# Row-wise cosine similarity: loading the last tiles in chunks and storing the result as transposed rows

## The chip, the cores and the metric

The kernel runs on one core of a Trainium2 chip. The metric is the device time of one execution in microseconds, given as the median over the executions of a kernel. It is about 1.8 us longer than the span of the same execution in the profile (before: profiled run 1284.43 us, span 1282.6 us); the span is what the profile's views divide up.

## The reference

```python
def setup_inputs():
    return {"x": np.random.randn(8192, 8192).astype(np.float32),
            "y": np.random.randn(8192, 8192).astype(np.float32)}

def reference(x, y):
    x_norm = np.linalg.norm(x, axis=1, keepdims=True)
    y_norm = np.linalg.norm(y, axis=1, keepdims=True)
    return np.sum(x * y, axis=1) / (x_norm.squeeze() * y_norm.squeeze() + 1e-8)
```

Each of 8192 rows gives one number. 537 MB are read and 32 KB are written.

## The kernel before

The rows are cut into 64 tiles of 128 rows, one row per partition. Each tile of x and of y is one 4 MB load. ScalarE squares and sums x and y, and VectorE multiplies and sums x·y. Each tile leaves one column of `sxx`, `syy` and `sxy`. At the end a short chain turns the three [128x64] arrays into results, and one DMA stores them. In that store, neighbouring elements of a partition lie 128 elements apart in memory, so it consists of 8192 pieces of four bytes.

```python
    data = ctx.enter_context(tc.tile_pool(name="data", bufs=2))
    ...  # cut: other pools, sxx, syy, sxy [128, 64], bf16 scratch
    for i in range(ntiles):
        xt = data.tile([P, D], fp32)
        yt = data.tile([P, D], fp32)
        nc.sync.dma_start(out=xt, in_=x[i * P : (i + 1) * P, :])
        nc.sync.dma_start(out=yt, in_=y[i * P : (i + 1) * P, :])
        nc.scalar.activation(out=act_scr, in_=xt, func=Square, accum_out=sxx[:, i : i + 1])
        nc.scalar.activation(out=act_scr, in_=yt, func=Square, accum_out=syy[:, i : i + 1])
        nc.vector.tensor_tensor_reduce(out=dve_scr, in0=xt, in1=yt, ..., accum_out=sxy[:, i : i + 1])
    ...  # cut: den = sxx*syy; sqrt; +1e-8; reciprocal; res = sxy*rec, all [128, 64]
    out_v = out.rearrange("(i p) -> p i", p=P)
    nc.sync.dma_start(out=out_v, in_=res)
```

Of the kernel before, what the change touches and what calls it, by code (L numbers as in the profile page):

```python
# [1 line left out]

# [4 lines left out]


@with_exitstack
def kernel(  # L10
    ctx: ExitStack,
    tc: tile.TileContext,
    x: bass.AP,
    y: bass.AP,
    out: bass.AP,
):
    nc = tc.nc
    P = nc.NUM_PARTITIONS
    N, D = x.shape
    ntiles = (N + P - 1) // P  # L20
    assert N % P == 0

    fp32 = mybir.dt.float32
    bf16 = mybir.dt.bfloat16

    data = ctx.enter_context(tc.tile_pool(name="data", bufs=2))
    scratch = ctx.enter_context(tc.tile_pool(name="scratch", bufs=1))
    stats = ctx.enter_context(tc.tile_pool(name="stats", bufs=1))

    sxx = stats.tile([P, ntiles], fp32)  # L30
    syy = stats.tile([P, ntiles], fp32)
    sxy = stats.tile([P, ntiles], fp32)

    act_scr = scratch.tile([P, D], bf16)
    dve_scr = scratch.tile([P, D], bf16)

    for i in range(ntiles):
        xt = data.tile([P, D], fp32)
        yt = data.tile([P, D], fp32)
        nc.sync.dma_start(out=xt, in_=x[i * P : (i + 1) * P, :])  # L40
        nc.sync.dma_start(out=yt, in_=y[i * P : (i + 1) * P, :])  # L41

        nc.scalar.activation(  # L43
            out=act_scr,
            in_=xt,
            func=mybir.ActivationFunctionType.Square,
            accum_out=sxx[:, i : i + 1],
        )
        nc.scalar.activation(  # L49
            out=act_scr,  # L50
            in_=yt,
            func=mybir.ActivationFunctionType.Square,
            accum_out=syy[:, i : i + 1],
        )
        nc.vector.tensor_tensor_reduce(  # L55
            out=dve_scr,
            in0=xt,
            in1=yt,
            scale=1.0,
            scalar=0.0,  # L60
            op0=mybir.AluOpType.mult,
            op1=mybir.AluOpType.add,
            accum_out=sxy[:, i : i + 1],
        )

    den = stats.tile([P, ntiles], fp32)
    nc.vector.tensor_tensor(out=den, in0=sxx, in1=syy, op=mybir.AluOpType.mult)  # L67
    sden = stats.tile([P, ntiles], fp32)
    nc.scalar.activation(  # L69
        out=sden, in_=den, func=mybir.ActivationFunctionType.Sqrt  # L70
    )
    sdene = stats.tile([P, ntiles], fp32)
    nc.vector.tensor_single_scalar(  # L73
        out=sdene, in_=sden, scalar=1e-8, op=mybir.AluOpType.add
    )
    rec = stats.tile([P, ntiles], fp32)
    nc.vector.reciprocal(out=rec, in_=sdene)  # L77
    res = stats.tile([P, ntiles], fp32)
    nc.vector.tensor_tensor(out=res, in0=sxy, in1=rec, op=mybir.AluOpType.mult)  # L79

    out_v = out.rearrange("(i p) -> p i", p=P)
    nc.sync.dma_start(out=out_v, in_=res)


# [1 line left out]
_INS = ['x', 'y']  # L86
_OUTS = [((8192,), 'float32')]


# [23 lines left out]
```

## Time and profile before

| | before |
|---|---|
| median (first 4 runs) | 1284.81 us |
| span of the profiled run | 1282.6 us |
| last y tile lands | 1248.4 us |
| from there to the end (the tail) | 34.2 us |

These are lines of the profile's page of the kernel before: busy time of the engines, packets, the load queue, the chain that ended last, the largest group of VectorE, and the output store with its median time from issue to landing. (Issue is the moment at which an engine hands a DMA over, landing the moment at which its last completion signal arrives; a packet is one piece of it, here one row of a load or one element of the old store.)

```profile
DVE 557.9 (43%) x132; ACT 914.5 (71%) x259; POOL 0.2 (0%) x4
...
DMA packets 26648, 536.97 MB, mean 419 GB/s; under 512 B 10257, under 2 KB 10257, under 8 KB 10257
...
q1 hardware_dynamic: 26640, 536.91, 99.0%
...
DMA 75%; DVE 22%; SPq 1%; issue 1%; DVEq 0%; ACT 0%
...
L55 DVE CUSTOM_DVE_ANT_0 dve_scr<-xt,yt 128x8192 bf16<-128x8192 f32 x64 | 556.3, 8692 | 700.5 <-DMA yt<-in_y_dram 700.5
...
out_dram<-res SPq DMA_DIRECT2D x1, 32.0 KB, 23.0
```

Neither compute engine is near its limit; the DMA engines are. The table by stretches of the span (columns: stretch, length, busy time of DVE, ACT and POOL, clock, DMA share, GB/s) shows where the load stream runs and where it doesn't:

```profile
20.00:600.00 580.00, 261.00 (x60) 423.55 (x120) 0.00 (x0) 1.00 1.00 432
600.00:1200.00 600.00, 269.70 (x62) 438.56 (x125) 0.00 (x0) 1.00 1.00 432
...
1248.50:1282.60 34.10, 9.81 (x6) 8.66 (x4) 0.00 (x0) 1.00 0.65 1
```

For 1180 us the stream is saturated at 432 GB/s. In the last 34 us the DMA engines are busy 65% of the time and move 1 GB/s: that is the output store. The timeline (start, duration, engine, line, operation, and in brackets the idle time before it with its releaser) shows what the tail is made of:

```profile
1248.60 8.69 DVE L55 CUSTOM_DVE_ANT_0 dve_scr<-xt,yt 128x8192 bf16<-128x8192 f32 x1 [10.93 <-DMA yt<-in_y_dram]
1255.66 1.28 ACT L69 ACT_TABLE_LOAD   x1
1257.21 0.22 DVE L67 TENSOR_TENSOR den<-sxx,syy 128x64 f32<-128x64 f32 x1
...
1258.57 0.23 DVE L79 TENSOR_TENSOR res<-sxy,rec 128x64 f32<-128x64 f32 x1
1258.82 0.41 SPq L82 DMA_DIRECT2D out_dram<-res  x1
```

### The profile page before, as it was taken

What the parts mean: (1) busy time and instruction counts of PE and PEld (TensorE: products, weight loads), DVE (VectorE), ACT (ScalarE), POOL (GpSimd) and SP (SyncE); (2) the same over time, 40 slices, a digit from 0 to 9 for tenths busy, and PEclk for the clock granted to TensorE, in tenths of its full rate; (3) what the DMA queues carried; (4) which work ended last, traced back from release to release, by engine and by line L of the source; (5) the groups of instructions that cost most, each with busy time, mean ns of one, the idle gap of its engine ahead of it and who ended that gap; (6) DMA issues with size and microseconds to landing.
All of it is one profiled execution on the core that took longest, in us unless ns stands there. A gap on an engine that the chain in (4) does not pass through costs nothing.

```text
span 1282.6 us, 881 instructions
## 1 busy us (share of the span) xinstructions
DVE 557.9 (43%) x132; ACT 914.5 (71%) x259; POOL 0.2 (0%) x4
## 2 busy tenths in 40 slices
DVE  2345344354354353453453453543543534534532
ACT  4777777677677767767777776776777777677672
POOL 0000000000000000000000000000000000000000
DMA  9999999999999999999999999999999999999986
GB/s 409 425 441 425 434 432 427 438 426 435 431 430 434 427 437 429 430 434 427 440 426 432 433 427 439 426 436 430 426 439 426 438 427 430 436 427 436 428 364 1
DMA packets 26648, 536.97 MB, mean 419 GB/s; under 512 B 10257, under 2 KB 10257, under 8 KB 10257
## 3 DMA queue, kind: packets, MB, share of 16 engines
q1 hardware_dynamic: 26640, 536.91, 99.0%
q14 instruction: 8, 0.06, 0.0%
HBM read 536.87 MB, written 0.03 MB: 419 GB/s over the span
## 4 chain that ended last, share of the span: by engine, by line
DMA 75%; DVE 22%; SPq 1%; issue 1%; DVEq 0%; ACT 0%
DMA yt<-in_y_dram 75%; DVE dve_scr L55 22%; SPq L40 1%; DVEq L55 0%; SPq L41 0%; DVE sxy L55 0%; DVE rec L77 0%; ACT sden L69 0%; DVE res L79 0%; DVE sdene L73 0%; DVE den L67 0%
## 5 line engine op out<-in xcount | busy, mean ns | idle before, releaser
L55 DVE CUSTOM_DVE_ANT_0 dve_scr<-xt,yt 128x8192 bf16<-128x8192 f32 x64 | 556.3, 8692 | 700.5 <-DMA yt<-in_y_dram 700.5
L43 ACT ACTIVATE act_scr<-xt 128x8192 bf16<-128x8192 f32 x64 | 449.9, 7029 | 175.9 <-DMA xt<-in_x_dram 175.9
L49 ACT ACTIVATE act_scr<-yt 128x8192 bf16<-128x8192 f32 x64 | 449.9, 7030 | 166.1 <-DMA yt<-in_y_dram 166.1
L49 ACT ACTIVATION_READ_ACCUMULATOR act_scr<-yt 128x1 f32 x64 | 11.9, 186 | 0.0
L43 ACT ACTIVATION_READ_ACCUMULATOR act_scr<-xt 128x1 f32 x64 | 11.9, 186 | 0.0
L55 DVE DVE_READ_ACCUMULATOR2_ANT sxy<- 128x1 f32 x64 | 5.3, 83 | 0.0
L43 ACT ACT_TABLE_LOAD x1 | 1.3, 1283 | 0.7 <-PEq L97 0.7
L69 ACT ACT_TABLE_LOAD x1 | 1.3, 1283 | 0.0
L69 ACT ACTIVATE sden<-den 128x64 f32<-128x64 f32 x1 | 0.3, 256 | 0.5 <-DVE den L67 0.5
L77 DVE RECIPROCAL rec<-sdene 128x64 f32<-128x64 f32 x1 | 0.6, 554 | 0.0
L73 DVE TENSOR_SCALAR sdene<-sden 128x64 f32<-128x64 f32 x1 | 0.2, 194 | 0.3 <-ACT sden L69 0.3
L79 DVE TENSOR_TENSOR res<-sxy,rec 128x64 f32<-128x64 f32 x1 | 0.2, 225 | 0.0
L67 DVE TENSOR_TENSOR den<-sxx,syy 128x64 f32<-128x64 f32 x1 | 0.2, 219 | 0.0
L97 POOL MEMSET const-bfloat16-1.0<- 128x1 bf16 x1 | 0.1, 101 | 0.0
L97 POOL MEMSET const-uint8-127<- 128x1 uint8 x1 | 0.1, 101 | 0.0
L97 POOL MEMSET const-float32-0.0<- 128x1 f32 x1 | 0.1, 98 | 0.2 <-issue 0.2
L97 POOL MEMSET const-float32-1.0<- 128x1 f32 x1 | 0.1, 98 | 0.0
## 6 DMA issues: line engine op xcount, KB each, us to landing
xt<-in_x_dram SPq DMA_DIRECT2D x64, 4096.0 KB, 20.2
yt<-in_y_dram SPq DMA_DIRECT2D x64, 4096.0 KB, 29.5
out_dram<-res SPq DMA_DIRECT2D x1, 32.0 KB, 23.0
```

What stands on the lines that cost most here:

```text
L40: nc.sync.dma_start(out=xt, in_=x[i * P : (i + 1) * P, :])
L43: nc.scalar.activation(out=act_scr, in_=xt, func=mybir.ActivationFunctionType.Square, accum_out=sxx[:, i : i + 1],)
L49: nc.scalar.activation(out=act_scr, in_=yt, func=mybir.ActivationFunctionType.Square, accum_out=syy[:, i : i + 1],)
L55: nc.vector.tensor_tensor_reduce(out=dve_scr, in0=xt, in1=yt, scale=1.0, scalar=0.0, op0=mybir.AluOpType.mult, op1=mybir.AluOpType.add, ac ...
L67: nc.vector.tensor_tensor(out=den, in0=sxx, in1=syy, op=mybir.AluOpType.mult)
L69: nc.scalar.activation(out=sden, in_=den, func=mybir.ActivationFunctionType.Sqrt)
L73: nc.vector.tensor_single_scalar(out=sdene, in_=sden, scalar=1e-8, op=mybir.AluOpType.add)
L77: nc.vector.reciprocal(out=rec, in_=sdene)
L79: nc.vector.tensor_tensor(out=res, in0=sxy, in1=rec, op=mybir.AluOpType.mult)
L97: nc = _bacc.Bacc("TRN2", target_bir_lowering=False, num_devices=1)
```

## The change

Its intent is to shorten what follows the last load. The last tile is loaded and reduced in chunks of 2048, 2048, 2048, 1024 and 1024 columns (the one before it in two halves), so that little work is left when the last bytes land. The first 63 result columns are finished, transposed on TensorE and stored while the last tile loads. At the end only one column remains; it is transposed into one 512-byte row. A first square root on ScalarE makes it load the activation table once, at the start.

```diff
+    def chunks_of(t):
+        plan = {ntiles - 2: [4096, 4096],
+                ntiles - 1: [2048, 2048, 2048, 1024, 1024]}
+        ...
+    def emit_early():                      # columns 0..62
+            ...                            # the same chain as before, 63 wide
+            nc.tensor.transpose(res_t_ps, res[:, 0:M], ident)
+            nc.vector.tensor_copy(out=res_t, in_=res_t_ps)
+            nc.sync.dma_start(out=out_v[0:M, :], in_=res_t)
 ...
+        for (s, e) in bnds:
+            nc.sync.dma_start(out=xt[:, s:e], in_=x[t * P : (t + 1) * P, s:e])
+            yq.dma_start(out=yt[:, s:e], in_=y[t * P : (t + 1) * P, s:e])
+        if t == ntiles - 1:
+            emit_early()
+        if first:
+            make_identity(nc, ident)
+            nc.vector.memset(warm, 1.0)
+            nc.scalar.sqrt(out=warm, in_=warm)
+        for k, (s, e) in enumerate(bnds):
+            ...                            # squares and product per chunk, partial sums in csxx, csyy, csxy
 ...
+    nc.vector.reduce_sum(out=a, in_=csxx[:, c0:c1], axis=mybir.AxisListType.X)
+    ...                                    # csyy, csxy; the chain on [128, 1] -> res1
+    nc.tensor.transpose(row_ps, res1, ident)
+    nc.vector.tensor_copy(out=row, in_=row_ps)
+    nc.scalar.dma_start(out=out_v[t : t + 1, :], in_=row)
-    out_v = out.rearrange("(i p) -> p i", p=P)
-    nc.sync.dma_start(out=out_v, in_=res)
```

More of the change, by code (lines that the diff above doesn't have):

```diff
@@ L5 @@
 from concourse import bass_utils, mybir
+from concourse.masks import make_identity
 from concourse._compat import with_exitstack
@@ L24 @@
     bf16 = mybir.dt.bfloat16
+    AX = mybir.AluOpType
+    def chunks_of(t):
+        plan = {
+            ntiles - 2: [4096, 4096],
+            ntiles - 1: [2048, 2048, 2048, 1024, 1024],
+        }
+        ws = plan.get(t, [D])
+        assert sum(ws) == D
+        bounds = []
+        s = 0
+        for w in ws:
+            bounds.append((s, s + w))
+            s += w
+        return bounds
+    consts = ctx.enter_context(tc.tile_pool(name="consts", bufs=1))
     data = ctx.enter_context(tc.tile_pool(name="data", bufs=2))
@@ L28 @@
     stats = ctx.enter_context(tc.tile_pool(name="stats", bufs=1))
+    psum = ctx.enter_context(tc.tile_pool(name="psum", bufs=1, space=bass.MemoryType.PSUM))
     sxx = stats.tile([P, ntiles], fp32)
@@ L32 @@
     sxy = stats.tile([P, ntiles], fp32)
+    NCH = 24
+    csxx = stats.tile([P, NCH], fp32)
+    csyy = stats.tile([P, NCH], fp32)
+    csxy = stats.tile([P, NCH], fp32)
     act_scr = scratch.tile([P, D], bf16)
     dve_scr = scratch.tile([P, D], bf16)
-    for i in range(ntiles):
+    ident = consts.tile([P, P], fp32)
+    warm = consts.tile([1, 1], fp32)
+    out_v = out.rearrange("(i p) -> i p", p=P)
+    coff = {}
+    off = 0
+    for t in range(ntiles):
+        b = chunks_of(t)
+        if len(b) > 1:
+            coff[t] = off
+            off += len(b)
@@ new lines @@
+    assert off <= NCH
+    def emit_early():
+            M = ntiles - 1
+            den = stats.tile([P, ntiles], fp32)
+            nc.vector.tensor_tensor(out=den[:, 0:M], in0=sxx[:, 0:M], in1=syy[:, 0:M], op=AX.mult)
+            sden = stats.tile([P, ntiles], fp32)
+            nc.scalar.activation(out=sden[:, 0:M], in_=den[:, 0:M], func=mybir.ActivationFunctionType.Sqrt)
+            rec = stats.tile([P, ntiles], fp32)
+            nc.vector.tensor_single_scalar(out=rec[:, 0:M], in_=sden[:, 0:M], scalar=1e-8, op=AX.add)
+            nc.vector.reciprocal(out=rec[:, 0:M], in_=rec[:, 0:M])
+            res = stats.tile([P, ntiles], fp32)
+            nc.vector.tensor_tensor(out=res[:, 0:M], in0=sxy[:, 0:M], in1=rec[:, 0:M], op=AX.mult)
+            res_t_ps = psum.tile([M, P], fp32)
+            nc.tensor.transpose(res_t_ps, res[:, 0:M], ident)
+            res_t = stats.tile([M, P], fp32)
+            nc.vector.tensor_copy(out=res_t, in_=res_t_ps)
+            nc.sync.dma_start(out=out_v[0:M, :], in_=res_t)
@@ L38 @@
+    first = True
+    for t in range(ntiles):
         xt = data.tile([P, D], fp32)
         yt = data.tile([P, D], fp32)
-        nc.sync.dma_start(out=xt, in_=x[i * P : (i + 1) * P, :])
-        nc.sync.dma_start(out=yt, in_=y[i * P : (i + 1) * P, :])
-        nc.scalar.activation(
-            out=act_scr,
-            in_=xt,
-            func=mybir.ActivationFunctionType.Square,
-            accum_out=sxx[:, i : i + 1],
-        )
-        nc.scalar.activation(
-            out=act_scr,
-            in_=yt,
-            func=mybir.ActivationFunctionType.Square,
-            accum_out=syy[:, i : i + 1],
-        )
@@ L55 @@
-        nc.vector.tensor_tensor_reduce(
-            out=dve_scr,
-            in0=xt,
-            in1=yt,
-            scale=1.0,
-            scalar=0.0,
-            op0=mybir.AluOpType.mult,
-            op1=mybir.AluOpType.add,
-            accum_out=sxy[:, i : i + 1],
-        )
-    den = stats.tile([P, ntiles], fp32)
-    nc.vector.tensor_tensor(out=den, in0=sxx, in1=syy, op=mybir.AluOpType.mult)
-    sden = stats.tile([P, ntiles], fp32)
-    nc.scalar.activation(
-        out=sden, in_=den, func=mybir.ActivationFunctionType.Sqrt
-    )
@@ L72 @@
-    sdene = stats.tile([P, ntiles], fp32)
-    nc.vector.tensor_single_scalar(
-        out=sdene, in_=sden, scalar=1e-8, op=mybir.AluOpType.add
-    )
-    rec = stats.tile([P, ntiles], fp32)
-    nc.vector.reciprocal(out=rec, in_=sdene)
-    res = stats.tile([P, ntiles], fp32)
-    nc.vector.tensor_tensor(out=res, in0=sxy, in1=rec, op=mybir.AluOpType.mult)
-    out_v = out.rearrange("(i p) -> p i", p=P)
-    nc.sync.dma_start(out=out_v, in_=res)
+        bnds = chunks_of(t)
+        yq = nc.sync
@@ new lines @@
+        for (s, e) in bnds:
[4 more added lines that the diff above has]
+        if first:
+            first = False
+            make_identity(nc, ident)
+            nc.vector.memset(warm, 1.0)
+            nc.scalar.sqrt(out=warm, in_=warm)
+        for k, (s, e) in enumerate(bnds):
+            if len(bnds) == 1:
+                axx, ayy, axy = sxx[:, t : t + 1], syy[:, t : t + 1], sxy[:, t : t + 1]
+            else:
+                c = coff[t] + k
+                axx, ayy, axy = csxx[:, c : c + 1], csyy[:, c : c + 1], csxy[:, c : c + 1]
+            nc.scalar.activation(
+                out=act_scr[:, s:e],
+                in_=xt[:, s:e],
+                func=mybir.ActivationFunctionType.Square,
+                accum_out=axx,
+            )
+            nc.scalar.activation(
+                out=act_scr[:, s:e],
+                in_=yt[:, s:e],
+                func=mybir.ActivationFunctionType.Square,
+                accum_out=ayy,
+            )
+            nc.vector.tensor_tensor_reduce(
+                out=dve_scr[:, s:e],
+                in0=xt[:, s:e],
+                in1=yt[:, s:e],
+                scale=1.0,
+                scalar=0.0,
+                op0=AX.mult,
+                op1=AX.add,
+                accum_out=axy,
+            )
@@ new lines @@
+        if len(bnds) > 1 and t != ntiles - 1:
+            c0, c1 = coff[t], coff[t] + len(bnds)
+            nc.vector.reduce_sum(out=sxx[:, t : t + 1], in_=csxx[:, c0:c1], axis=mybir.AxisListType.X)
+            nc.vector.reduce_sum(out=syy[:, t : t + 1], in_=csyy[:, c0:c1], axis=mybir.AxisListType.X)
+            nc.vector.reduce_sum(out=sxy[:, t : t + 1], in_=csxy[:, c0:c1], axis=mybir.AxisListType.X)
+    t = ntiles - 1
+    nb = len(chunks_of(t))
+    c0, c1 = coff[t], coff[t] + nb
+    fin = stats.tile([P, 8], fp32)
@@ new lines @@
+    a = fin[:, 0:1]
+    b = fin[:, 1:2]
+    c = fin[:, 2:3]
+    nc.vector.reduce_sum(out=a, in_=csxx[:, c0:c1], axis=mybir.AxisListType.X)
+    nc.vector.reduce_sum(out=b, in_=csyy[:, c0:c1], axis=mybir.AxisListType.X)
+    nc.vector.reduce_sum(out=c, in_=csxy[:, c0:c1], axis=mybir.AxisListType.X)
+    d = fin[:, 3:4]
+    nc.vector.tensor_tensor(out=d, in0=a, in1=b, op=AX.mult)
+    sd = fin[:, 4:5]
+    nc.scalar.activation(out=sd, in_=d, func=mybir.ActivationFunctionType.Sqrt)
+    r = fin[:, 5:6]
@@ L86 @@
+    nc.vector.tensor_single_scalar(out=r, in_=sd, scalar=1e-8, op=AX.add)
+    nc.vector.reciprocal(out=r, in_=r)
+    res1 = fin[:, 6:7]
+    nc.vector.tensor_tensor(out=res1, in0=c, in1=r, op=AX.mult)
+    row_ps = psum.tile([1, P], fp32)
+    nc.tensor.transpose(row_ps, res1, ident)
+    row = stats.tile([1, P], fp32)
+    nc.vector.tensor_copy(out=row, in_=row_ps)
+    nc.scalar.dma_start(out=out_v[t : t + 1, :], in_=row)
 _INS = ['x', 'y']
```

## The prediction

> **What bounds it now.** The load stream. The page's queue line gives the 16 DMA engines 99% of the span; the windows table shows 432 GB/s at a DMA share of 1.00 from 20 to 1200 us. The chain of waits is 75% "DMA yt" and 22% DVE, but that DVE share is a buffer release: a tile takes 19.4 us, of which ScalarE works 14.4 and VectorE 8.8, and its loads are issued when 9.7 us of y are still queued. The stream never starves. What it does not cover is the tail. By the timeline the last y tile lands at 1248.5 us and the span ends at 1282.6: 34.1 us, namely 8.7 us of VectorE multiply-reduce on the whole tile, 1.6 us of the final [128x64] chain, 23.0 us from issue to landing of the output DMA (8192 four-byte elements), and under 1 us of ending.
>
> **What changes, costed.**
> 1. Output. 63 of 64 columns are transposed on TensorE and stored as 512-byte rows while the last tile loads; one 512-byte row is left. The Trainium skill, "DMA: Bandwidth & Descriptors", Specifications, says writes below 512 B are read-modify-write; the 23.0 us here agrees in direction. The old store's first packet began about 1.45 us after its issue. I estimate 2.1 us for the new one: -20.9 us.
> 2. Last tile in chunks, the last of 1024 columns. Scaling 8.69 us by size with the fixed part kept gives 1.2 us for the VectorE piece. The program order puts the sum of the x partials before it, so it waits for ScalarE's last x square; I estimate it ends 2.1 us after the landing instead of 8.8: -6.7 us.
> 3. Added at the end: three small sums, a transpose, a PSUM copy, about 0.45 + 0.45 + 0.3 us; against narrower operations in the chain, +0.7 us net.
> 4. Chunk loads: 10 more DMAs and rows of 4 to 16 KB for 32 KB. A 32 KB packet takes 1.218 us and packets follow without gaps: 0 to 1 us, say +0.5. By the landing times several chunks are still queued when the last are issued: no starvation.
> 5. One activation table load instead of two (the skill, "ScalarE: Activation LUTs", What ACT_TABLE_LOAD costs: 1283 ns; the trace agrees, 1283 ns): the second was hidden behind VectorE, worth 0. The early output block runs on idle engines: 0.
>
> Sum: -20.9 - 6.7 + 0.7 + 0.5 = -26.4 us, all on the critical path. The stream, 97% of the time, is untouched.
>
> **Predicted: 1258.4 us, 8 in 10 between 1256.8 and 1260.2.** The 2% line is at 1259.1, so: faster 0.63, same 0.36, slower 0.01.
>
> **What would show each step.** (1) The last store lands about 2 us after issue; packets under 512 B fall from 10257 to about 2300. (2) The last VectorE product takes 1.2 us and ends 2 us after the last landing. (3) From its end to the last store's issue about 2.2 us. (4) The last y chunk lands at 1248.5 to 1249.5. (5) One table load, at the start. Tail: about 7.2 us against 34.1.
>
> **What would make it wrong.** A gap in the stream from the chunked issue, or slow small rows (over 1 us); a single-row store of 3 us or more; ScalarE lagging the 1024-column chunks (1.14 us of work against 1.22 us of load); the early block holding an engine into the last chunks; a slow first use of TensorE.

## The result and the profile after

The changed kernel takes 1256.58 us in the median (1256.35 to 1256.86, 8 runs), against 1284.29 us (1283.51 to 1285.72, 12 runs) for the kernel before. The ratio is 0.9783, with a 95% interval from 0.9773 to 0.9793. Ratios here are the mean time of one kernel's fast runs over that of the other's of the same rounds, so not quite the ratio of the medians. The direction was predicted and the time was not: 1256.58 us lies 0.22 us under the stated range, and the gain is 27.7 us where 26.4 us were forecast.

The page of the changed kernel, the lines that answer to those above:

```profile
PE 0.8 (0%) x2; PEld 0.3 (0%) x2; DVE 560.4 (45%) x155; ACT 915.9 (73%) x280; POOL 0.7 (0%) x6
...
DMA packets 19953, 536.97 MB, mean 428 GB/s; under 512 B 2218, under 2 KB 2282, under 8 KB 2794
...
q1 hardware_dynamic: 19944, 536.91, 99.5%
...
L107 ACT ACT_TABLE_LOAD x1 | 1.3, 1283 | 0.7 <-PEq L182 0.7
```

The table by stretches of the changed kernel (columns: stretch, length, busy PE, PE weight load, DVE, ACT, POOL, clock, DMA share, GB/s):

```profile
20.00:600.00 580.00, 0.00 (x0) 0.00 (x0) 261.01 (x60) 423.85 (x121) 0.00 (x0) 1.00 1.00 432
600.00:1200.00 600.00, 0.00 (x0) 0.00 (x0) 269.72 (x62) 438.11 (x124) 0.00 (x0) 1.00 1.00 432
...
1249.20:1255.00 5.80, 0.37 (x1) 0.08 (x1) 2.37 (x10) 1.71 (x5) 0.00 (x0) 1.00 0.00 0
```

The stream is the same 432 GB/s, and the tail is 5.8 us. The timeline of that tail:

```profile
1248.42 1.04 ACT L115 ACTIVATE act_scr<-xt 128x1024 bf16<-128x1024 f32 x1
...
1249.59 1.06 ACT L121 ACTIVATE act_scr<-yt 128x1024 bf16<-128x1024 f32 x1
1249.59 0.16 DVE L151 TENSOR_REDUCE fin<-csxx 128x1 f32<-128x5 f32 x1 [1.46 <-ACT act_scr L115]
1249.71 1.23 DVE L127 CUSTOM_DVE_ANT_0 dve_scr<-xt,yt 128x1024 bf16<-128x1024 f32 x1
...
1251.05 0.15 DVE L155 TENSOR_TENSOR fin<-fin 128x1 f32<-128x1 f32 x1
...
1252.07 0.37 PE L164 MATMUL row_ps<-ident,fin 128*1 128x128 f32 x1 [13.29 <-DVE fin L162]
1252.48 0.28 DVE L166 COPY row<-row_ps 1x128 f32<-1x128 f32 x1 [0.47 <-PE row_ps L164]
1252.80 0.49 ACTq L167 DMA_DIRECT2D out_dram<-row  x1
```

VectorE did not wait for the last y chunk, which landed at 1249.19 us. It waited 1.46 us for ScalarE's last x square, because the sum of the x partials stands ahead of the last product on VectorE; only the last 0.4 us of this wait (1249.19 to 1249.59) lie behind the landing. The waits of SyncE say when the last store landed: SyncE finished its own last issue at 1239.5 us and then waited 14.4 us for the row.

```profile
SPq L193 <- DMA out_dram<-row: 14.4, 1, 14.4
```

That puts the landing at 1253.9 us, which is also the last landing that the trace records (1253.90). From these times the difference of the two spans can be added up:

| piece | before, us | after, us | measured change | predicted |
|---|---|---|---|---|
| start to landing of the last y | 1248.44 | 1249.19 | +0.75 | +0.5 |
| landing to end of the last product | 8.85 | 1.75 | -7.10 | -6.7 |
| product to issue of the last store | 1.53 | 1.86 | +0.33 | +0.7 |
| store, issue to landing | 22.97 | 1.10 | -21.87 | -20.9 |
| landing to end of span | 0.85 | 1.09 | +0.24 | 0 |
| sum | 1282.65 | 1254.99 | -27.65 | -26.4 |

The table compares one trace of each kernel. The largest miss, 1.0 us, is the store.

One thing about the end of the stream is easily overlooked. The semaphore of the last y load counts 16 completion signals. In the changed kernel 13 of them had come by 1247.42 us, and the last three came at 1248.49, 1248.88 and 1249.19. Before the change it was 1246.41, then 1247.58, 1248.22 and 1248.44. So in both kernels the last three signals come 1.1 to 2.0 us after the others, and the tail starts with the very last.

### The profile page after: what moved, and what is told of

It is laid out like the page before. It is cut to its first block, busy times and chain, and to the rows that moved or that the text cites. A ratio compares the mean times of both kernels' runs of the same rounds, so it can differ in the third digit from the quotient of the medians.

```text
span 1255.0 us, 956 instructions
## 1 busy us (share of the span) xinstructions
PE 0.8 (0%) x2; PEld 0.3 (0%) x2; DVE 560.4 (45%) x155; ACT 915.9 (73%) x280; POOL 0.7 (0%) x6
## 4 chain that ended last, share of the span: by engine, by line
DMA 76%; DVE 22%; SPq 1%; issue 1%; ACT 0%; DVEq 0%; PE 0%; ACTq 0%
DMA yt<-in_y_dram 76%; DVE dve_scr L127 22%; SPq L97 1%; ACT act_scr L121 0%; SPq L98 0%; ACT act_scr L115 0%; DVEq L127 0%; DVE sxy L127 0%; PE row_ps L164 0%; DVE row L166 0%; ACT fin L157 0%; DVE fin L160 0%; DVE fin L162 0%; DVE fin L159 0%; DVE fin L153 0%
## 5 line engine op out<-in xcount | busy, mean ns | idle before, releaser
L127 DVE CUSTOM_DVE_ANT_0 dve_scr<-xt,yt 128x8192 bf16<-128x8192 f32 (+3 forms) x69 | 557.1, 8073 | 683.6 <-DMA yt<-in_y_dram 683.6
L115 ACT ACTIVATE act_scr<-xt 128x8192 bf16<-128x8192 f32 (+3 forms) x69 | 450.8, 6534 | 170.5 <-DMA xt<-in_x_dram 170.4
L121 ACT ACTIVATE act_scr<-yt 128x8192 bf16<-128x8192 f32 (+3 forms) x69 | 450.9, 6535 | 163.8 <-DMA yt<-in_y_dram 163.7
```

What stands on the lines that cost most here:

```text
L115: nc.scalar.activation(out=act_scr[:, s:e], in_=xt[:, s:e], func=mybir.ActivationFunctionType.Square, accum_out=axx,)
L121: nc.scalar.activation(out=act_scr[:, s:e], in_=yt[:, s:e], func=mybir.ActivationFunctionType.Square, accum_out=ayy,)
L127: nc.vector.tensor_tensor_reduce(out=dve_scr[:, s:e], in0=xt[:, s:e], in1=yt[:, s:e], scale=1.0, scalar=0.0, op0=AX.mult, op1=AX.add, accu ...
```

## The experiments

Twelve kernels were run. All gave correct results.

### Which part of the change earns what, and what sets the store's time

**Store only.** The kernel before with the transposed store.

```diff
 ...                                                   # cut: ident, PSUM pool and tiles
-    out_v = out.rearrange("(i p) -> p i", p=P)
-    nc.sync.dma_start(out=out_v, in_=res)
+    nc.tensor.transpose(res_t_ps, res, ident)         # [64, 128]
+    nc.vector.tensor_copy(out=res_t, in_=res_t_ps)
+    nc.sync.dma_start(out=out.rearrange("(i p) -> i p", p=P), in_=res_t)
```

> The kernel before with one edit: all 64 result columns are transposed on TensorE and stored as 64 rows of 512 bytes, at the end; loads, tiles and chain unchanged. Theory A (the store's cost follows the number of its packets; one small store costs about 1.1 us, 64 rows about 1.4 us): the store lands about 1.4 us after its issue, transpose and copy add 0.9 us, so the gain is 23.0 - 1.4 - 0.9 = 20.7 us, time about 1263.6 us. Theory B (the cost follows the queue: the row store was quick because it alone used ScalarE's queue; from SyncE, behind 128 loads, about 2.1 us as predicted): gain about 20.0 us, store about 2.1 us.

Measured: 1264.05 us against 1283.70 us, ratio 0.9846 (0.9833 to 0.9860). The issue line of its page:

```profile
out_dram<-res_t SPq DMA_DIRECT2D x1, 32.0 KB, 1.8
```

The store's 1.8 us lie between the two theories (1.4 and 2.1 us), and the gain of 19.7 us is a little below both (20.7 and 20.0); this run alone does not tell them apart. It does show that the shape of the store alone is worth 19.7 us, the transpose and copy that it needs included.

**Chunks only.** The chunked loads of the changed kernel, no early block, one 64-wide chain at the end and the old scattered store.

```diff
-        if t == ntiles - 1:
-            emit_early()
 ...
-    nc.scalar.dma_start(out=out_v[t : t + 1, :], in_=row)
+    nc.sync.dma_start(out=out.rearrange("(i p) -> p i", p=P), in_=res)
```

> The changed kernel's chunked loads, but nothing finished early and the old scattered store of [128x64] at the end. If the parts add: the last product ends 1.75 us after the last landing instead of 8.8, the landing is 0.75 us later, the partial sums add about 0.4 us: gain about 5.9 us, time about 1278.4 us, store still 23.0 us. If the chunks' gain existed only together with the early block (rival): gain under 3 us.

Measured: 1280.12 us (1278.22 to 1280.50), ratio 0.9967 (0.9955 to 0.9980). The profiled run was the fastest of the five (span 1276.4 us, 6.2 us under the profile of before), and in it the parts add as expected. The median gain is 3.6 us, less than the 5.9 us expected. Kernels with the scattered store vary by more than 2 us from run to run (the kernel before: 1282.38 to 1285.10 in these rounds), and why the other four runs here were slower than the profiled one is left open. The pair without that store answers the question better: from "store only" (1264.05 us) to "no early block" (1258.32 us, next) the chunks are the only difference that counts, and they are worth 5.7 us. (The table load at the start also differs, but in "store only" the late one ran from 1255.4 to 1256.7 us, while VectorE worked on its last product until 1257.0.)

**No early block.** Chunks, one 64-wide chain and one transposed store of 64 rows at the end.

```diff
-        if t == ntiles - 1:
-            emit_early()
 ...
+    nc.tensor.transpose(res_t_ps, res, ident)         # all 64 columns, at the end
+    ...                                               # cut: the copy from PSUM
+    nc.sync.dma_start(out=out.rearrange("(i p) -> i p", p=P), in_=res_t)
```

> The changed kernel without the early block: chunks, and at the end one 64-wide chain and one transposed store of 64 rows. The narrow chain at the end saves only about 0.5 us of arithmetic and 0.3 us of store: expect 0.8 to 1.0 us slower than the changed kernel, about 1257.5 us. Rival (the early store is what matters): several us slower.

Measured: 1258.32 us, which is 1.8 us slower than the kernel of the same rounds that keeps the block (next, 1256.51 us). The early block earns 1.8 us, not the 0.8 to 1.0 us expected. The trace shows how: the chain from the last product to the issue takes 2.58 us instead of 1.86, and the 64-row store takes 1.86 us instead of 1.10. So 0.72 + 0.76 = 1.5 us of it are seen in those two pieces; the store's share was put too low. The rest is within the scatter of the load stream from trace to trace (see "Tile 62 whole again").

**The last row from SyncE's queue.**

```diff
-    nc.scalar.dma_start(out=out_v[t : t + 1, :], in_=row)
+    nc.sync.dma_start(out=out_v[t : t + 1, :], in_=row)
```

> The changed kernel with its last 512-byte row stored from SyncE's queue, which carried all the loads, instead of ScalarE's. Theory A (packets): issue to landing stays 1.1 us, time the same within 0.3 us. Theory B (queue): issue to landing about 2 us, time about 0.9 us longer.

Measured: 1256.51 us (1256.41 to 1256.64); issue to landing 1.09 us. The queue is not the reason why the row store was quicker than estimated. Theory B fell.

**The last column stored without a transpose.**

```diff
-    nc.tensor.transpose(row_ps, res1, ident)
-    nc.vector.tensor_copy(out=row, in_=row_ps)
-    nc.scalar.dma_start(out=out_v[t : t + 1, :], in_=row)
+    out_c = out.rearrange("(i p) -> p i", p=P)
+    nc.scalar.dma_start(out=out_c[:, t : t + 1], in_=res1)
```

> The changed kernel without the last transpose and PSUM copy: the last [128x1] result goes out straight from its 128 partitions, as 128 four-byte packets. The issue comes about 0.77 us earlier. Theory A (cost follows the number of packets): the store takes longer than the row's 1.1 us, about like the 64-row store's 1.8 us or up to 2.2 us, so the time is the same to 0.3 us longer. Rival (any tiny store costs the same 1.1 us): 0.77 us shorter.

Measured: 1261.88 us, 5.3 us slower than the changed kernel; both theories missed. The issue line:

```profile
out_dram<-fin ACTq DMA_DIRECT2D x1, 0.5 KB, 6.5
```

The same 512 bytes cost 1.1 us as one row and 6.5 us as 128 four-byte pieces. The packet records say where: the first packet ran 0.86 us after the issue, all were done 1.07 us after it, and the landing came 5.46 us after the last packet. The old store shows the same wait: its last packet ended 4.52 us before its landing. For the row it is 0.33 us, for the 64 rows 0.35 us. Theory A (number of packets) is therefore incomplete: a large part of the cost is a wait after the last packet. In the old store the packets still count for most: its 23.0 us are 0.98 to the first packet, 17.5 of packets and 4.5 of wait.

**Two stores of 256-byte packets.** This asks whether that wait comes with every packet under 512 bytes.

```diff
-    nc.sync.dma_start(out=out_v, in_=res_t)
+    nc.sync.dma_start(out=out_v[:, 0:64], in_=res_t[:, 0:64])
+    nc.sync.dma_start(out=out_v[:, 64:128], in_=res_t[:, 64:128])
```

> The store-only kernel (old loads, 64 transposed columns stored at the end) with its store cut into two of 64 packets of 256 bytes each. Theory R (writes under 512 bytes are slow to be confirmed, whatever their number: the old store landed 4.5 us after its last packet, the 128 four-byte packets 5.4 us after theirs, the 512-byte rows 0.3 us after): the second store lands over 4 us after its last packet, time about 4 to 6 us longer than the store-only kernel, about 1269 us. Rival C (the wait comes with four-byte packets, 256 bytes are large enough): only the second issue and 64 more packets, time 0.3 to 0.8 us longer, about 1264.6 us.

Measured: 1264.72 us, 0.7 us over "store only" (from another call). The issue line shows both stores at 1.8 us, and the second landed 0.35 us after its last packet.

```profile
out_dram<-res_t SPq DMA_DIRECT2D x2, 16.0 KB, 1.8
```

Rival C holds: 256 bytes are large enough to escape the wait. The number of packets is hardly the cause either: 128 went out here in two stores, as many as in the column store. Nothing between 4 and 256 bytes was run. One rival stands untested: in both four-byte stores, pieces from different partitions lie side by side in memory, 128 of them in one row of 512 bytes. Whether the wait comes from the size of the pieces or from this neighbourhood, no run separates.

### What sets the end of the load stream, and the work behind it

**Every tile in rows of 16 KB.**

```diff
-        ws = plan.get(t, [D])
+        ws = plan.get(t, [4096, 4096])
 ...                                     # cut: more columns for the partial sums
```

> The changed kernel with every tile loaded as two halves, so rows of 16 KB in place of 32 KB throughout. Theory P (every packet costs about 14 ns besides its bytes: the trace of the changed kernel shows 1217.5 ns for 32 KB, 615.9 for 16 KB, 314.0 for 8 KB, 162.7 for 4 KB): 992 more packets per engine times 14.3 ns is 14.2 us more, time about 1270.8 us, with the DMA share still 1.00. Rival E (the 0.75 us later landing is a start or end effect of the chunked tiles and not of packets): within 1 us of the changed kernel.

Measured: 1268.66 us (1268.64 to 1268.87), 12.1 us slower than the changed kernel. The stretches of this run:

```profile
20.00:600.00 580.00, 0.00 (x0) 0.00 (x0) 271.88 (x208) 438.22 (x237) 0.00 (x0) 1.00 1.01 428
600.00:1200.00 600.00, 0.00 (x0) 0.00 (x0) 280.77 (x212) 453.42 (x246) 0.00 (x0) 1.00 1.01 428
```

The DMA share is 1.01 and the rate falls from 432 to 428 GB/s, so the queue did not run dry; the packets themselves cost more: two of 16 KB take 2 x 615.1 ns in the mean, one of 32 KB in the changed kernel 1217.5. From the first load packet to the end of the last one the stream is 12.18 us longer, over 992 extra packets per engine: 12.3 ns each. That holds for the last of the 16 completion signals, which sets the time; the median one came 9.2 us later than in the changed kernel. Rival E fell, and theory P was 2 us too high in size. In the change under study the chunked tiles have 80 extra packets per engine (16 for tile 62, 64 for tile 63). At 12.3 ns that is an estimate of 0.98 us, against 0.78 us by which the stream grew (0.86 us between the means of the seven traces with these loads and the three with the loads of before).

**Tile 62 whole again.**

```diff
-            ntiles - 2: [4096, 4096],
```

> The changed kernel with tile 62 loaded and computed whole again (only the last tile in chunks). Theory L (ScalarE's lag paces the tail): ScalarE starts tile 63 about 5 us late behind 7.2 us of work on y of tile 62 and catches up only about 0.4 us per half-chunk, so its last x square ends about 2.2 us later than 1249.6 us: time about 2.2 us longer, about 1258.7 us. Rival S (only the stream counts, and 16 fewer, larger packets per engine save 0.2 us): time about 0.2 us shorter.

Measured: 1258.29 us, 1.7 us slower than the changed kernel, although the stream was not longer (0.33 us shorter in these two traces; in seven traces with the loads of the changed kernel it took 1246.65 to 1247.38 us, so a difference of this size between two traces means little). Timeline lines of this run:

```profile
1228.77 7.03 ACT L120 ACTIVATE act_scr<-yt 128x8192 bf16<-128x8192 f32 x1 [2.59 <-DMA yt<-in_y_dram]
1235.93 1.91 ACT L114 ACTIVATE act_scr<-xt 128x2048 bf16<-128x2048 f32 x1
...
1251.11 0.16 DVE L150 TENSOR_REDUCE fin<-csxx 128x1 f32<-128x5 f32 x1 [3.38 <-ACT act_scr L114]
```

ScalarE enters the last tile at 1235.9 us instead of 1233.0, doesn't catch up, and VectorE waits 3.38 us for it at the end instead of 1.46. Theory L holds (expected +2.2 us, measured +1.7): the halves of tile 62 are needed for ScalarE. What they cost the stream, this run does not show.

**The last x square on VectorE.**

```diff
+            if t == ntiles - 1 and k == len(bnds) - 1:
+                nc.vector.tensor_tensor_reduce(out=dve_scr[:, s:e], in0=xt[:, s:e], in1=xt[:, s:e], ..., accum_out=axx)
+            else:
                 nc.scalar.activation(..., func=Square, accum_out=axx)
```

> The changed kernel with the x square of the last 1024 columns moved from ScalarE to VectorE. Theory L (ScalarE's lag holds the last product back, by the x partial that is summed before it): the last product ends 0.3 to 0.4 us earlier, time about 1256.2 us. Rival (the landing of the last y chunk paces it): no change, within 0.1 us, or slower by the added VectorE work.

Measured: 1256.54 us (1256.10 to 1256.83): no change in the median. In the profiled run the last product ended 1.46 us after the landing instead of 1.75, in line with theory L, but the five runs spread over 0.73 us, more than twice the effect. Inconclusive.

**x in rows of 64 KB.** If packets have a fixed cost, larger ones should help. In 30 tiles of 256 rows, two adjacent rows of x lie in one partition; to make room, ScalarE's scratch is fp8 and both scratches are 4096 wide.

```diff
+        xv = x[r0 : r0 + 2 * P, :].rearrange("(p r) d -> p (r d)", r=2)
 ...   # cut: yv, the same view of y
+        xt = data.tile([P, 2 * D], fp32, tag="x")
+        nc.sync.dma_start(out=xt, in_=xv)
+        for r in range(2):
+            yt = data.tile([P, D], fp32, tag="y")
+            nc.sync.dma_start(out=yt, in_=yv[:, r, :])
 ...   # results of the two rows are transposed apart and interleaved in the PSUM copy
```

> A rewritten kernel after the packet law: 30 tiles of 256 rows, two adjacent rows of x in one partition, so x comes in rows of 64 KB (y still in rows of 32 KB), the last four tiles and the tail as in the changed kernel, columns stored early as far as they are done. Theory P (each packet costs 12.3 ns besides its bytes, from the 16 KB run): 240 fewer packets per engine, 2.95 us less stream, time about 1253.6 us. Rival (no packet over 32 KB, or no gain beyond it): 1256.5 us or more. It would also be slower if ScalarE or VectorE, now with longer bursts of work, let the queue run dry; the windows would show a DMA share under 1.00.

Measured: 1257.52 us, 0.9 us slower than the changed kernel had been. The trace shows 3840 packets of 64 KB. From 20 to 1200 us their mean is 2422.9 ns, against 2 x 1217.0 ns for two of 32 KB in the changed kernel, so 11.1 ns saved each. The stream was 1.06 us shorter, not 2.95, and the tail was 7.7 us instead of 5.8. The packet times say 240 x 11.1 ns = 2.7 us per engine; only 1.1 us of that reaches the end of the stream. The completion signals of the last y load say where the rest went: the median of the 16 came 2.3 us earlier than in the changed kernel (1244.92 against 1247.22 us), the last only 1.05 us earlier, because two of them came at 1247.77 and 1248.14. Why those two lag further here is left open. The longer tail had a visible cause: VectorE waited longer for ScalarE's last x square, and the next run mends that.

```profile
1250.63 0.16 DVE L142 TENSOR_REDUCE fin<-lxx 128x1 f32<-128x5 f32 x1 [3.43 <-ACT act_scr L54]
```

**The same with ScalarE's order mended, and the changed kernel beside it.**

```diff
+            if t < ntiles - 2:              # tiles 60 and 61: both x halves before y
+                if k == 0:
+                    for h in range(2):
+                        sq(xt[:, h * H : (h + 1) * H], pxx[:, t, h : h + 1])
+            else:
                 sq(xt[:, a:b], axx)
```

> The 64 KB kernel with one fault of mine mended: in tiles 60 and 61 ScalarE squared the second half of x only after y had landed, so it entered the chunks about 3.7 us late, and its last x square ended 2.4 us after the last landing instead of 0.4. With both x halves squared before y, theory L (ScalarE's lag paces the tail) expects the tail back near that of the changed kernel (5.8 us from last landing to end, against 7.6 now), with the stream 1.1 us shorter: about 1255.7 us. If the longer tail came from something else of the 64 KB form: about 1257.5 us again.

> The changed kernel itself, on the same chip and in the same rounds, to compare with the 64 KB kernel: about 1256.5 us, spread under 0.6 us.

Measured in the same rounds: the mended 64 KB kernel 1255.96 us (1255.79 to 1256.01, ratio 0.9777), the changed kernel 1256.65 us (1256.55 to 1256.90, ratio 0.9782). The tail is back at 5.9 us, so theory L holds here too. The 64 KB kernel is 0.7 us faster than the changed one; the two ranges don't overlap, but it is 0.05% for a much longer kernel. VectorE's wait in the mended one:

```profile
1248.77 0.16 DVE L147 TENSOR_REDUCE fin<-lxx 128x1 f32<-128x5 f32 x1 [1.76 <-ACT act_scr L54]
```

## Why the prediction was right or wrong

- **What bounds the kernel: right.** The stream is 432 GB/s at a share of 1.00 in both traces, and the gain is the tail's (34.2 to 5.8 us).
- **Step 1, the store, was the step that failed, by its size.** The prediction said: "The old store's first packet began about 1.45 us after its issue. I estimate 2.1 us for the new one: -20.9 us." The new store takes 1.10 us (0.73 us to the first packet, 0.04 us of packets, 0.33 us to the landing), so the term is -21.87 us. Part of the miss was a faulty reading: with the packet records put on the span's clock rightly, the old store's first packet began 0.98 us after its issue, and the new one's came sooner still. For what follows the first packet the estimate leaves 0.65 us, and it took 0.37; the prediction does not say what it put there. The old store was no measure for it: 4.5 us pass from its last packet to the landing, 0.3 us for rows. That the queue is not the reason is shown by the run from SyncE; that the four-byte form is the expensive one is shown by the column store (6.5 us) against the row (1.1 us), though not whether by the size of its pieces or by their place.
- **Step 2, the last product: right in mechanism, 0.4 us too little.** It was said to end 2.1 us after the landing, held back by the sum of the x partials; it ended 1.75 us after, held back by exactly that.
- **Step 3, the added operations: 0.4 us too much.** From product to issue it took 1.86 us, not 2.2.
- **Step 4, the chunked loads: right.** +0.75 us against +0.5, within the stated 0 to 1, and no starvation: the DMA share is 1.00 up to 1200 us and 0.99 from there to 1246. The 16 KB run shows that the cost belongs to packets.
- **Step 5: right as a cost.** There is one table load, at the start, and the early block did not delay the loads: the stream without it was no shorter (1247.38 us, against 1246.99). But a 0 for the block hides what it buys: without it the kernel is 1.8 us slower. That worth was inside step 1's one-row store and the narrower chain. What the early square root is worth was not tested alone.
- **The range.** Three terms erred the same way (1.0 + 0.4 + 0.4 us) and two against them (0.25 + 0.24 us), which leaves 1.25 us, less than the 1.6 us that the range allowed below the forecast. The other 0.5 us came from the starting point: the forecast of 1258.4 us was taken from 1284.81 us, the median of the first four runs of the kernel before, and the median of all twelve is 1284.29. With that start the result would have lain inside the range, so that it lies 0.22 us outside is partly chance.

## What to carry to other kernels

When a kernel is saturated by its loads, look at what follows the last landing and add it up piece by piece: work on the last tile, chain, store, ending. Make the last piece of work small, keep every engine caught up before it, and store in contiguous rows; here the form of 32 KB of output was worth 19.7 us and the chunks 5.7 us. Split a DMA's time into issue to first packet, packets, and last packet to landing before using one store to estimate another: in these runs the first part went from 0.7 to 1.2 us, the second from 0.04 to 18 us and the third from 0.3 to 5.5 us, and they did not move together.

## What the Trainium skill lacked or had wrong

- "DMA: Bandwidth & Descriptors", Specifications, sets line rate at 512 bytes and says that smaller writes are read-modify-write. That threshold does not mark the wait at the end of a kernel: packets of 256 bytes landed 0.35 us after the last one, just as 512-byte rows did (0.32 to 0.36 us). With four-byte packets the landing came 4.0 to 5.5 us after the last, even for only 128 of them. For DMAs that GpSimd issues, the page speaks of a wait until the last byte is confirmed, but it has no figure for a wait that depends on the size of the pieces.
- The same page, Latency and other measured facts, gives about 600 ns to the first byte for such queues. The runs show, counted from the start of the issue, 0.72 to 0.75 us for one row, from either queue, and 1.18 to 1.19 us for 64 rows.
- The same page, Why small descriptors are slow, speaks of a fixed overhead of about 3 cycles a packet, which matters for small ones; the page's nearest figure in time is about 10.5 ns a packet, for a 4 KB transfer issued from GpSimd. The runs show 12.3 ns per packet (by the end of the stream), and it is visible even at 16 KB rows: 12.2 us of the stream. From 32 KB to 64 KB a packet grows by 1205.9 ns; 16 engines at that pace make 434.8 GB/s (an estimate), which agrees with the 435.2 GB/s of its section Where 436 GB/s comes from.
- No page says that a scattered store also makes times uneven: the kernels with 8192 four-byte pieces spread over 1.6 to 3.6 us within one set of rounds, the others over 0.8 us or less.
